# A weights-stationary projection as three 256-column matmuls into a half bank, instead of 512 + 256 columns whose halves are added afterwards

## The chip, the core and the metric

The kernel runs on one core of a Trainium2 chip. The metric is the device time of one execution in microseconds (us); the time before is the median of three runs.

## What is computed

The reference is a two-layer decoder trunk on 256 tokens (`T`) with 2048 features (`D_MODEL`). Layer 0 normalises, multiplies by one wide input matrix, runs an mLSTM head group and an SSD (state-space) head group, and projects back. Layer 1 is causal attention with 16 heads and rotary positions. Each layer ends in a SwiGLU feed-forward network of width 5632. All inputs and outputs are float32.

```python
def swiglu(x, w_gate, w_up, w_down):
    return (jax.nn.silu(x @ w_gate) * (x @ w_up)) @ w_down
...
    proj = (xn @ w_in).astype(f32)                  # layer 0: q, k, v, o, gates, z, x/B/C
...
    qkv = (xn @ w_qkv).astype(jnp.float32)          # layer 1
```

Nearly all the work is in these products `x @ w`.

## The kernel before

**Precision.** Both factors of a product are split into two parts of the type float32r: a high part and the rest. With x = xh + xl and w = wh + wl, the kernel adds three products, wh xh + wh xl + wl xh. The class `KT` (L140 to L158) holds an operand with its features on the partitions; its blocks keep xh and xl of a feature tile side by side, 256 tokens each, so that `both(k)` (L156) is one row of 512 columns [xh | xl] and `parts(k)` (L151) gives the two apart.

**Weights.** `chunk` (L192) brings 2 x 128 rows of a strip of 512 columns of a weight matrix in by DMA from the SP queue (`raw`, 512 KB), has ScalarE (ACT) copy it to `wh` (L202) and VectorE (DVE) subtract to get `wl` (L203). There are four buffers of `raw`, three each of `wh` and `wl`. These two steps are emitted with a raised priority.

**The two forms of a product.** `lin_a` (L234) keeps the activations stationary and moves 512 weight columns per matmul, three matmuls (L247 to L249) per feature tile and token tile. `lin_w` (L206) keeps the weights stationary. It makes a strip of 512 output features in four banks of PSUM, one for each 128 features, over 16 feature tiles k of the input, so it issues 4 x 16 = 64 pairs of matmuls per strip. The first of a pair (L217) multiplies `wh` with the 512 columns [xh | xl] into the whole bank, the second (L219) multiplies `wl` with the 256 columns xh into the first half of the bank:

```python
banks = [acc_bank("acc_w") for _ in range(4)]
...
nc.tensor.matmul(banks[f], wh[:, kk, fs], kt.both(k), start=k == 0, ...)
nc.tensor.matmul(banks[f][:, :T], wl[:, kk, fs], kt.parts(k)[0], start=False, ...)
```

**Reading the sums.** At the end of a strip the two halves of each bank are still to be added. `lin_sum` (L224) copies the second half to SBUF on ACT (L225) and adds the first half on VectorE (L226). `lin_scaled` (L228) does that and multiplies by the norm's factor by token on VectorE (L232).

**Who calls `lin_w`.** 64 strips: four for q and k of layer 0 (L278 and L328), eight in `conv_strip` (L484, four of x and two each of B and C), 44 in the two `ffn` (L626: 11 gate strips, read by `lin_scaled`, and 11 up strips, read by `lin_sum` and a product L648, in each), eight in `rope_strip` (L665, read by `lin_sum`, then by products L673 and L677 with the rotary factors and by the ACT copies L675 and L676 that swap halves).

**The gates.** The 96 gate columns of layer 0 are a product of their own (L343 to L345), weights stationary, 16 feature tiles of `xa`, three matmuls of 256 columns each, all into one half of a bank: `wgh` by xh, `wgh` by xl, `wgl` by xh.

**Order of the work.** PSUM has six banks with the tag `acc` (`psa`, for `lin_w` and `lin_a`) and two with the tag `aux` (for transposes and small products). Small pieces of work (transposes, mLSTM heads, SSD heads, attention heads) are not emitted where they come up: `later` puts them on a list, due some chunks of weights later, and `tick` (L133), called after every chunk, emits what is due. They thus run between the matmuls of the projections. Each engine works its queue in order.

Of the kernel before, what the change touches and what calls it, by code (L numbers as in the profile page):

```python
# [17 lines left out]
P = 128  # L18
T = 256
# [5 lines left out]
KC = 2  # L25
# [28 lines left out]
def hybrid_trunk(ctx: ExitStack, tc: tile.TileContext, a: dict, out: bass.AP):  # L54
# [19 lines left out]
    def acc_bank(name):  # L74
        return psa.tile([P, 512], F32, tag="acc", name=name)
# [45 lines left out]
    def later(wait, name, fn, *args):  # L121
        """Emit fn(*args) behind the next wait chunks of weights."""
        pending.append((clock[0] + wait, len(pending), name, fn, args))
# [16 lines left out]
    class KT:  # L140
        """Features on partitions, split in two float32r parts, 4 tiles of 128 features to a block."""

# [17 lines left out]
    def transpose_split(kt, b, src, gcol, half):  # L160
        """src[t]: [128 tokens, 512 features] -> half of block b of kt, times the gains."""
        blk_ = kt.block(b)
        pt = aux_bank("p_tr")
        for j in range(2):
            for t in range(NT):
                c = (2 * half + j) * P
                nc.tensor.transpose(pt[:, j * T + t * P:j * T + (t + 1) * P], src[t][:, c:c + P], ident)  # L167
        for j in range(2):
            k = 2 * half + j
            split(blk_[:, k, 0, :], blk_[:, k, 1, :], pt[:, j * T:(j + 1) * T],  # L170
                  pv[:, gcol + 4 * b + k:gcol + 4 * b + k + 1])
# [5 lines left out]
    def row_norm(name, ss4):  # L177
        """r [128, 2] by token, 0.5 r, and r over the free dimension on all partitions [128, 256]."""
        ss = sml.tile([P, NT], F32, tag="ss", name="ss" + name)
        nc.vector.tensor_reduce(ss, ss4, axis=AX.X, op=OP.add)  # L180
        r = cst.tile([P, NT], F32, name="r" + name)
        rsqrt_mean(r, ss, D)
        pb = aux_bank("p_rb")
        for t in range(NT):
            dg = t2([P, P], "dg")
            nc.vector.tensor_scalar(dg, ident, r[:, t:t + 1], None, op0=OP.mult)
            nc.tensor.matmul(pb[:, t * P:(t + 1) * P], ones, dg, start=True, stop=True)
        rb = cst.tile([P, T], F32, tag="rb", name="rb" + name, bufs=2)
        nc.scalar.copy(rb, pb[:, :T])
        return r, rb  # L190

    def chunk(w, k, col, step=KC):  # L192
        """KC x 128 rows of a strip of w in two float32r parts, brought in and split step x 128 rows at a time."""
        raw = stg.tile([P, KC, STRIP], F32, tag="raw", name="raw", bufs=4)
        wh = stg.tile([P, KC, STRIP], F32R, tag="wh", name="wh")
        wl = stg.tile([P, KC, STRIP], F32R, tag="wl", name="wl")
        for i in range(0, KC, step):
            ks = slice(i, i + step)
            nc.sync.dma_start(raw[:, ks, :],
                              w[(k + i) * P:(k + i + step) * P, col:col + STRIP].rearrange("(a p) f -> p a f", p=P))  # L200
            with tc.high_priority(offset=800):
                nc.scalar.copy(wh[:, ks, :], raw[:, ks, :])  # L202
                nc.vector.tensor_sub(wl[:, ks, :], raw[:, ks, :], wh[:, ks, :].bitcast(F32))  # L203
        return wh, wl

    def lin_w(w, col, kt, nk, ready=None):  # L206
        """Weights stationary: a bank for 128 features, [w x_hi | w_hi x_lo], which adds up to [128, 256 tokens]."""
        banks = [acc_bank("acc_w") for _ in range(4)]
        for k0 in range(0, nk, KC):
            wh, wl = chunk(w, k0, col, KC if ready is None or k0 else 1)  # L210
            if ready is not None:
                ready(k0)
            for f in range(4):
                fs = slice(f * P, (f + 1) * P)
                for kk in range(KC):
                    k = k0 + kk
                    nc.tensor.matmul(banks[f], wh[:, kk, fs], kt.both(k), start=k == 0, stop=False,  # L217
                                     skip_group_check=True)
                    nc.tensor.matmul(banks[f][:, :T], wl[:, kk, fs], kt.parts(k)[0], start=False, stop=k == nk - 1,  # L219
                                     skip_group_check=True)  # L220
            tick()
        return banks

    def lin_sum(bank, dst):  # L224
        nc.scalar.copy(dst, bank[:, T:])  # L225
        nc.vector.tensor_add(dst, bank[:, :T], dst)  # L226

    def lin_scaled(bank, dst, rb):  # L228
        """dst = the product, times a factor by token."""
        s = t2([P, T], "ls")  # L230
        lin_sum(bank, s)
        nc.vector.tensor_mul(dst, s, rb)  # L232

    def lin_a(w, col, kt, nk, lead=1):  # L234
        """Activations stationary: [128 tokens, 512 features] in a bank per token tile."""
        banks = [acc_bank("acc_a") for _ in range(NT)]
# [19 lines left out]

    # ------------------------------------------------------------ layer 0 input
    w_in = a["l0_w_in"]
# [25 lines left out]
    nc.vector.tensor_scalar(rh0, r0_, 0.5, None, op0=OP.mult)  # L284
    for f in range(4):
        lin_scaled(banks_q[f], qT[:, f, :], rb0)

    # ------------------------------------------------------------ small parameters
    mask_sl = cst.tile([P, P], F32, name="mask_sl")
# [35 lines left out]

    # ------------------------------------------------------------ q, k
    for dst, c0, s in ((qT, C_Q, 1), (kT, C_K, 0), (kT, C_K, 1)):
        banks = lin_w(w_in, c0 + s * STRIP, xt0, KD)  # L328
        for f in range(4):
            lin_scaled(banks[f], dst[:, 4 * s + f, :], rb0)  # L330

    # ------------------------------------------------------------ gates
    wg = blk([P, KD, 96], "wg")
# [65 lines left out]
    def decay_rows(first):  # L399
        """Rows first .. first + 3 on all partitions, l in 0:256 and 128:256 again, masked on the diagonal blocks."""  # L400
        rb = blk([P, 4, W3], "rows4")
# [9 lines left out]
    def decay(row, bias):  # L411
        """exp(row[l] + bias[s]) for s <= l, 0 elsewhere: [128 s, (s tile 0: 256 l | s tile 1: 128 l)]."""
        e = t2([P, W3], "dec")
        nc.scalar.activation(e[:, :T], row[:, :T], AF.Exp, bias=bias[0])
        nc.scalar.activation(e[:, T:], row[:, T:], AF.Exp, bias=bias[1])
        return e

    # ------------------------------------------------------------ mLSTM
    v = [blk([P, MH, MDV + 1], f"v{t}") for t in range(NT)]
# [62 lines left out]

    # ------------------------------------------------------------ SSD
    def conv_strip(col, dst):  # L484
        """dst: [128 channels, 4, 256] <- silu(conv) of 512 channels."""
        banks = lin_w(w_in, C_X + col, xt0, KD)
        for b in range(2):
            xr = t2([P, 2, T + 3], "xr")
            nc.gpsimd.memset(xr[:, :, 0:3], 0.0)
            for j in range(2):  # L490
                lin_scaled(banks[2 * b + j], xr[:, j, 3:], rb0)
            cv = t2([P, 2, T], "cv")
# [112 lines left out]

    # ------------------------------------------------------------ residual blocks
    xr_ = [blk([P, D], f"xres{t}") for t in range(NT)]
# [3 lines left out]
    def project_add(w, kt, nk, name, gcol):  # L611
        """x += kt.T @ w; the next layer's operands, strip by strip, and its norm."""
        nx = KT("x" + name, KD)
# [12 lines left out]
    def ffn(xt, rb, wg_, wu_, name):  # L626
# [3 lines left out]
        for s in range(DFF // STRIP):  # L630
            banks = lin_w(wg_, s * STRIP, xt, KD)
            sgs = []
            for b in range(2):
                gs = t2([P, 2, T], "sg")
                sgs.append(gs)
                for j in range(2):
                    lin_scaled(banks[2 * b + j], gs[:, j, :], rbh)
                th = t2([P, 2, T], "thf")
# [5 lines left out]
            for b in range(2):  # L644
                ur = t2([P, 2, T], "ur")
                for j in range(2):
                    lin_sum(banks[2 * b + j], ur[:, j, :])
                nc.vector.tensor_mul(ur, ur, sgs[b])  # L648
                split(hb[:, 2 * b:2 * b + 2, 0, :], hb[:, 2 * b:2 * b + 2, 1, :], ur)
# [5 lines left out]

    # ------------------------------------------------------------ attention
    rope = cst.tile([P, 2, T], F32, name="rope")
# [7 lines left out]
    def rope_strip(col, name):  # L665
        banks = lin_w(w_qkv, col, xt2, KD)
        dst = blk([P, 4, T], name)
        for b in range(2):
            src = t2([P, 2, T], "rsrc")
            for j in range(2):  # L670
                lin_sum(banks[2 * b + j], src[:, j, :])
            d2 = dst[:, 2 * b:2 * b + 2, :]
# [61 lines left out]

    # ------------------------------------------------------------ last projection and norm
    gf = blk([P, D], "gf")
# [46 lines left out]
```

## Time and profile before

| | us |
|---|---|
| median of 3 runs | 2677.27 (2677.26 to 2678.13) |
| profiled execution, span from first to last instruction | 2676.2 |
| PE (TensorE matmuls) busy | 2655.2, 13765 matmuls |
| PEld (TensorE weight loads) busy | 2250.8, 13765 loads |
| DVE (VectorE) busy | 1621.3 |
| ACT (ScalarE) busy | 1334.3 |
| POOL (GpSimd) busy | 45.9 |

The profile gives the profiled execution's own time as its span, 2676.2 us; the median of the runs lies 1.1 us above it. Busy time is the time in which an engine had at least one instruction in work. Matmuls are pipelined: a matmul's record begins when it starts and ends when its modelled passage through the array is over, so records of neighbours overlap. The time from one start to the next shows the pace. Rows of a group of instructions read: line, engine, operation, what it writes `<-` what it reads, shapes, count | busy us, mean ns of one | idle time of the engine before them, and what ended it.

### The profile page before, as it was taken

The numbers are of one execution on the slowest core, as the hardware profiler recorded it, in microseconds if no ns is written. First come the engines' busy times: TensorE is split into PE (matmuls) and PEld (weight loads), VectorE is DVE, ScalarE is ACT, GpSimd is POOL, SyncE is SP. The second block draws the span as 40 slices with busy tenths as digits, with TensorE's granted clock in tenths as the row PEclk, the third lists the DMA queues.
The fourth block names the chain that finished last, engine by engine and source line by source line (L and its number), as shares of the span: only waits on it lengthen the run. The fifth ranks groups of instructions, "written<-read, shape, count | busy, mean of one in ns | idle before, by whom it ended". The sixth has DMA issues, their size and how long they took to land.

```text
span 2676.2 us, 35559 instructions
## 1 busy us (share of the span) xinstructions
PE 2655.2 (99%) x13765; PEld 2250.8 (84%) x13765; DVE 1621.3 (61%) x2128; ACT 1334.3 (50%) x1906; POOL 45.9 (2%) x97
## 2 busy tenths in 40 slices
PE   8999999999999999999999999999999999999998
PEld 7888888888888888888888888888888888888886
DVE  5675687755456666666544466566566666665454
ACT  5455665665444444444444455556444444444343
POOL 1000010000000000000000000000000000000000
PEclk9999999999999999999999999999999999999999
DMA  7566666566556666666655565554566666666664
GB/s 229 168 191 179 187 182 203 162 186 213 186 184 182 188 189 187 185 188 188 189 187 187 186 181 173 173 174 157 181 186 190 190 190 189 189 189 204 189 189 157
DMA packets 254344, 496.84 MB, mean 186 GB/s; under 512 B 15656, under 2 KB 16048, under 8 KB 253792
## 3 DMA queue, kind: packets, MB, share of 16 engines
q1 hardware_dynamic: 250816, 484.57, 60.2%
q0 software_dynamic: 2896, 8.51, 1.2%
q8 instruction: 107, 1.75, 0.3%
q10 hardware_dynamic: 464, 1.52, 0.2%
q14 instruction: 61, 0.50, 0.1%
HBM read 492.39 MB, written 2.14 MB: 185 GB/s over the span
## 4 chain that ended last, share of the span: by engine, by line
PE 98%; DVE 1%; DMA 1%; ACT 0%; issue 0%; POOL 0%; SPq 0%; ACTq 0%; POOLq 0%; DVEq 0%
PE acc_w L217 35%; PE acc_w L219 18%; PE acc_a L247 14%; PE acc_a L248 14%; PE acc_a L249 14%; PE p_tr L167 1%; PE p_y L572 1%; PE p_num L449 0%; DMA raw<-in_l_w_in 0%; DVE wl L203 0%; ACT wh L202 0%; PE p_qk L687 0%; PE p_o L717 0%; DMA xin<-in_x 0%; PE p_pt L709 0%
## 5 line engine op out<-in xcount | busy, mean ns | idle before, releaser
L203 DVE TENSOR_TENSOR wl<-raw,wh 128x1024 fp32r<-128x1024 f32 (+1 forms) x913 | 1117.4, 1224 | 947.8 <-ACT wh L202 944.2
L202 ACT CAST wh<-raw 128x1024 fp32r<-128x1024 f32 (+1 forms) x913 | 957.3, 1049 | 1171.2 <-PE acc_w L217 549.6
L217 PE MATMUL acc_w<-x,wh 128*128 128x512 f32 x3328 | 1168.8, 396 | 0.0
L219 PE MATMUL acc_w<-x,wl 128*128 128x256 f32 x3328 | 931.0, 280 | 0.0
L217 PEld LDWEIGHTS acc_w<-x,wh 128*128 128x128 f32 x3328 | 625.0, 188 | 146.0
L219 PEld LDWEIGHTS acc_w<-x,wl 128*128 128x128 f32 x3328 | 625.7, 188 | 0.5
L217 PE MATMUL acc_w<-xa,wh 128*128 128x512 f32 x768 | 275.5, 401 | 1.1 <-DVE xa L116 1.1
L219 PE MATMUL acc_w<-xa,wl 128*128 128x256 f32 x768 | 217.1, 285 | 0.0
L217 PEld LDWEIGHTS acc_w<-xa,wh 128*128 128x128 f32 x768 | 145.1, 189 | 33.1 <-ACT wh L202 1.5
L247 PE MATMUL acc_a<-wh,xa 128*128 128x512 f32 x384 | 152.9, 398 | 0.0
L248 PE MATMUL acc_a<-wl,xa 128*128 128x512 f32 x384 | 152.7, 398 | 0.0
L249 PE MATMUL acc_a<-wh,xa 128*128 128x512 f32 x384 | 152.3, 397 | 0.0
L219 PEld LDWEIGHTS acc_w<-xa,wl 128*128 128x128 f32 x768 | 145.3, 190 | 1.1
L247 PE MATMUL acc_a<-wh,ha 128*128 128x512 f32 x352 | 139.4, 396 | 0.0
L248 PE MATMUL acc_a<-wl,hb 128*128 128x512 f32 x352 | 139.0, 395 | 0.0
L247 PE MATMUL acc_a<-wh,hb 128*128 128x512 f32 x352 | 138.7, 394 | 0.0
L249 PE MATMUL acc_a<-wh,ha 128*128 128x512 f32 x352 | 138.7, 394 | 0.0
L249 PE MATMUL acc_a<-wh,hb 128*128 128x512 f32 x352 | 138.6, 394 | 0.0
L248 PE MATMUL acc_a<-wl,ha 128*128 128x512 f32 x352 | 138.5, 393 | 0.0
L247 PE MATMUL acc_a<-wh,mx 128*128 128x512 f32 x256 | 101.8, 397 | 0.0
L248 PE MATMUL acc_a<-wl,mx 128*128 128x512 f32 x256 | 101.1, 395 | 0.0
L249 PE MATMUL acc_a<-wh,mx 128*128 128x512 f32 x256 | 101.0, 394 | 0.0
(240 smaller groups left out, 2519.3 us busy)
## 6 DMA issues: line engine op xcount, KB each, us to landing
raw<-in_l_w_in SPq DMA_DIRECT2D x191, 512.0 KB, 3.7
raw<-in_l_ffn_gate SPq DMA_DIRECT2D x176, 512.0 KB, 3.7
raw<-in_l_ffn_up SPq DMA_DIRECT2D x176, 512.0 KB, 3.7
raw<-in_l_ffn_down SPq DMA_DIRECT2D x176, 512.0 KB, 4.4
raw<-in_l_w_qkv SPq DMA_DIRECT2D x96, 512.0 KB, 3.7
raw<-in_l_w_out SPq DMA_DIRECT2D x64, 512.0 KB, 3.8
raw<-in_l_w_o SPq DMA_DIRECT2D x32, 512.0 KB, 3.7
rows<-scr POOLq DMA_DIRECT2D x10, 512.0 KB, 6.4
```

Source lines behind the costliest of these rows:

```text
L167: nc.tensor.transpose(pt[:, j * T + t * P:j * T + (t + 1) * P], src[t][:, c:c + P], ident)
L202: nc.scalar.copy(wh[:, ks, :], raw[:, ks, :])
L203: nc.vector.tensor_sub(wl[:, ks, :], raw[:, ks, :], wh[:, ks, :].bitcast(F32))
L217: nc.tensor.matmul(banks[f], wh[:, kk, fs], kt.both(k), start=k == 0, stop=False, skip_group_check=True)
L219: nc.tensor.matmul(banks[f][:, :T], wl[:, kk, fs], kt.parts(k)[0], start=False, stop=k == nk - 1, skip_group_check=True)
L247: nc.tensor.matmul(banks[t], xh[:, ts], wh[:, kk, :], start=k == 0, stop=False)
L248: nc.tensor.matmul(banks[t], xh[:, ts], wl[:, kk, :], start=False, stop=False)
L249: nc.tensor.matmul(banks[t], xl[:, ts], wh[:, kk, :], start=False, stop=k == nk - 1)
L572: nc.tensor.matmul(py[:, o0:o0 + SHD], e[:, lo:lo + P], y[st][:, hs], start=st == 0, stop=st == t, skip_group_check=True)
```

## The change

`lin_w` takes two banks for a strip instead of four, two groups of 128 features to a bank, one in each half. For each group and feature tile it issues three matmuls of 256 columns into the same half bank: `wh` by xh, `wh` by xl, `wl` by xh. The three products are added in PSUM as they come. `lin_sum` is gone. `lin_scaled` is one VectorE product of 512 columns (two groups of features) that reads the bank; the up strips' product L648 and the rotary products and copies read the bank too. Comments and docstrings that the diff also touches are left out here.

```diff
     def lin_w(w, col, kt, nk, ready=None):
-        banks = [acc_bank("acc_w") for _ in range(4)]
+        banks = [acc_bank("acc_w") for _ in range(2)]
...
             for f in range(4):
                 fs = slice(f * P, (f + 1) * P)
+                o = banks[f // 2][:, (f % 2) * T:(f % 2 + 1) * T]
                 for kk in range(KC):
                     k = k0 + kk
-                    nc.tensor.matmul(banks[f], wh[:, kk, fs], kt.both(k), start=k == 0, stop=False,
+                    xh, xl = kt.parts(k)
+                    nc.tensor.matmul(o, wh[:, kk, fs], xh, start=k == 0 and f % 2 == 0, stop=False,
                                      skip_group_check=True)
-                    nc.tensor.matmul(banks[f][:, :T], wl[:, kk, fs], kt.parts(k)[0], start=False, stop=k == nk - 1,
-                                     skip_group_check=True)
+                    nc.tensor.matmul(o, wh[:, kk, fs], xl, start=False, stop=False, skip_group_check=True)
+                    nc.tensor.matmul(o, wl[:, kk, fs], xh, start=False, stop=k == nk - 1, skip_group_check=True)
             tick()
-        return banks
-
-    def lin_sum(bank, dst):
-        nc.scalar.copy(dst, bank[:, T:])
-        nc.vector.tensor_add(dst, bank[:, :T], dst)
+        return [b.rearrange("p (a b) -> p a b", a=2) for b in banks]
 
     def lin_scaled(bank, dst, rb):
-        s = t2([P, T], "ls")
-        lin_sum(bank, s)
-        nc.vector.tensor_mul(dst, s, rb)
+        nc.vector.tensor_mul(dst, bank, rb[:, None, :].to_broadcast([P, 2, T]))
...
     def conv_strip(col, dst):
-            for j in range(2):
-                lin_scaled(banks[2 * b + j], xr[:, j, 3:], rb0)
+            lin_scaled(banks[b], xr[:, :, 3:], rb0)
...
     def ffn(xt, rb, wg_, wu_, name):
-                for j in range(2):
-                    lin_scaled(banks[2 * b + j], gs[:, j, :], rbh)
+                lin_scaled(banks[b], gs, rbh)
...
-                for j in range(2):
-                    lin_sum(banks[2 * b + j], ur[:, j, :])
-                nc.vector.tensor_mul(ur, ur, sgs[b])
+                nc.vector.tensor_mul(ur, banks[b], sgs[b])
...
     def rope_strip(col, name):
-            src = t2([P, 2, T], "rsrc")
-            for j in range(2):
-                lin_sum(banks[2 * b + j], src[:, j, :])
+            src = banks[b]
```

The four q and k strips of layer 0 are read in the same way, by two `lin_scaled` of 512 columns instead of four of 256.

## Rows read from the trace of the kernel before

**Rows 1.** The page: busy time, share and count by engine; PE clock by slice.
```profile
PE 2655.2 (99%) x13765; PEld 2250.8 (84%) x13765; DVE 1621.3 (61%) x2128; ACT 1334.3 (50%) x1906; POOL 45.9 (2%) x97
...
PEclk9999999999999999999999999999999999999999
```

**Rows 2.** The page: the chain that ended last, shares by engine.
```profile
PE 98%; DVE 1%; DMA 1%; ACT 0%; issue 0%; POOL 0%; SPq 0%; ACTq 0%; POOLq 0%; DVEq 0%
```

**Rows 3.** Waits of PE: who waited for whom, us in total, times, longest.
```profile
PE p_rb L187 <- DVE dg L186: 2.6, 3, 0.9
PE acc_w L217 <- DVE xa L116: 1.1, 1, 1.1
PE p_cols L390 <- ACT colsrc L381: 0.7, 1, 0.7
PE acc_a L247 <- ACT wh L202: 0.5, 1, 0.5
PE p_xs L542 <- DVE xsT L503: 0.2, 1, 0.2
```

**Rows 4.** Groups of instructions on PE, by line and shape.
```profile
L217 PE MATMUL acc_w<-x,wh 128*128 128x512 f32 x3328 | 1168.8, 396 | 0.0
...
L217 PE MATMUL acc_w<-xa,wh 128*128 128x512 f32 x768 | 275.5, 401 | 1.1 <-DVE xa L116 1.1
```

**Rows 5.** Timeline of PE around the gates: start us, us, instruction.
```profile
83.59 0.39 PE L217 MATMUL acc_w<-xa,wh 128*128 128x512 f32 x1
...
105.95 0.28 PE L343 MATMUL p_gate<-xa,wgh 128*96 128x256 f32 x1
...
107.37 0.28 PE L343 MATMUL p_gate<-xa,wgh 128*96 128x256 f32 x1
...
108.76 0.28 PE L343 MATMUL p_gate<-xa,wgh 128*96 128x256 f32 x1
...
109.94 0.28 PE L344 MATMUL p_gate<-xa,wgh 128*96 128x256 f32 x1
...
110.55 0.28 PE L343 MATMUL p_gate<-xa,wgh 128*96 128x256 f32 x1
...
111.60 0.39 PE L217 MATMUL acc_w<-xa,wh 128*128 128x512 f32 x1
...
122.89 0.40 PE L217 MATMUL acc_w<-xa,wh 128*128 128x512 f32 x1
```

**Rows 6.** Timeline of PE in layer 0's feed-forward network, two strip starts.
```profile
820.65 0.39 PE L217 MATMUL acc_w<-x,wh 128*128 128x512 f32 x1
...
843.15 0.39 PE L217 MATMUL acc_w<-x,wh 128*128 128x512 f32 x1
```

**Rows 7.** Weight loads (PEld): timeline at 336 us, then two groups.
```profile
336.43 0.76 PEld L572 LDWEIGHTS p_y<-y,dec 128*128 128x128 f32 x6
337.10 0.19 PEld L217 LDWEIGHTS acc_w<-xa,wh 128*128 128x128 f32 x1
...
L248 PEld LDWEIGHTS acc_a<-wl,xa 128*128 128x128 f32 x384 | 72.2, 188 | 15.7
L247 PEld LDWEIGHTS acc_a<-wh,xa 128*128 128x128 f32 x384 | 72.2, 188 | 15.9
```

**Rows 8.** DMA queue of PE's instructions: packets, MB, share of 16 engines.
```profile
q8 instruction: 107, 1.75, 0.3%
```

**Rows 9.** Groups of instructions on ACT and DVE that read sums.
```profile
L225 ACT COPY ls<-acc_w 128x256 f32<-128x256 f32 x136 | 48.4, 365 | 6.9 <-PE acc_w L219 6.9
...
L226 DVE TENSOR_TENSOR ls<-acc_w,ls 128x256 f32<-128x256 f32 x136 | 55.1, 418 | 0.0
...
L648 DVE TENSOR_TENSOR ur<-ur,sg 128x512 f32<-128x512 f32 x44 | 30.2, 687 | 0.8
...
L232 DVE TENSOR_TENSOR sg<-ls,rbha 128x256 f32<-128x256 f32 x44 | 18.6, 424 | 1.1
...
L619 DVE TENSOR_TENSOR xres<-xres,acc_a 128x512 f32<-128x512 f32 x24 | 15.4, 681 | 0.0
```

More of the change, by code (lines that the diff above doesn't have):

```diff
@@ L284, in hybrid_trunk @@
     nc.vector.tensor_scalar(rh0, r0_, 0.5, None, op0=OP.mult)
-    for f in range(4):
-        lin_scaled(banks_q[f], qT[:, f, :], rb0)
+    for b in range(2):
+        lin_scaled(banks_q[b], qT[:, 2 * b:2 * b + 2, :], rb0)
     mask_sl = cst.tile([P, P], F32, name="mask_sl")
@@ L328, in hybrid_trunk @@
         banks = lin_w(w_in, c0 + s * STRIP, xt0, KD)
-        for f in range(4):
-            lin_scaled(banks[f], dst[:, 4 * s + f, :], rb0)
+        for b in range(2):
+            lin_scaled(banks[b], dst[:, 4 * s + 2 * b:4 * s + 2 * b + 2, :], rb0)
     wg = blk([P, KD, 96], "wg")
```

## The prediction

> **What bounds the kernel now.** I began with the page. TensorE is busy for 2655.2 of 2676.2 us and its clock is granted in full in every slice [rows 1]; the chain of work that ended last is 98% PE, 1% DVE and 1% DMA [rows 2]. A busy PE need not be a PE at its peak, so I next asked what it waits for. The waits that ACT or VectorE end are small: 2.6 us in three waits on `dg`, 1.1 on `xa`, 0.7 on `colsrc`, 0.5 on `wh`, 0.2 on `xsT`, 5.1 us in all [rows 3]; beside them that list has only two waits on input transfers at the very start. So the end is set by how fast PE takes its matmuls, and only that pace is worth reading closely.
>
> The changed code is that of 4096 pairs (3328 + 768), each a 512-column and a 256-column matmul on one bank [rows 4]. The durations there (396 and 401 ns) overlap and their ends are modelled, so the pace has to be read from starts. On layer 0's operand `xa`, the 64 pairs of a whole strip run from 83.59 to 105.95 us: 22.36 / 64 = 349.4 ns a pair. The next strip's first 32 pairs take 122.89 - 111.60 = 11.29 us, 352.8 ns a pair [rows 5]. In the feed-forward network of layer 0, 64 pairs take 22.50 us, 351.6 ns each [rows 6]. The same work thus differs by 3 ns from place to place.
>
> **The change part by part.**
>
> *The matmuls.* 512 + 256 columns become 3 x 256: the same 768 columns, but one more matmul and one more weight load per pair, 4096 of each. The kernel already has this form: the gates (L343 to L345) multiply hi by hi, hi by lo and lo by hi, 256 columns each, into one half bank. Their 16 triples run from 105.95 to 111.60 us: 5.65 / 16 = 353.1 ns [rows 5]. The moving tiles are the very same `xa`; only the weights are 96 columns wide instead of 128. Against the strip before, a triple is 353.1 - 349.4 = 3.7 ns dearer; against the mean of both neighbours, (349.4 + 352.8) / 2 = 351.1, it is 2.0 dearer. I take the middle, 2.8 ns: 4096 x 2.8 = **11.5 us more**, all on the path, since PE is the path. The ends: the gates' fastest four triples (107.37 to 108.76) take 347.5 ns each, 1.9 less than the strip before, which gives 4096 x -1.9 = -7.8 us; their slowest four (105.95 to 107.37) take 355.0, 5.6 more, +22.9 us [rows 5].
>
> The Trainium skill, page "TensorE: Matmul & The Clock Gate", section "Wait — 56ns, not 53.3ns?", says that every matmul costs some 2.5 ns beyond its columns at the full clock. By it the split would cost 4096 x 2.5 = 10.2 us, an estimate of that page; the 2.0 to 3.7 ns above agree with it.
>
> *The third load.* A load of 128 columns is recorded at 188 ns, but loads overlap in the record. Where they set the pace, before 64-column matmuls, six start between 336.43 and 337.10 us, one every 112 ns [rows 7]. A 256-column matmul takes 353.1 / 3 = 117.7 ns, so a load still fits behind each, with 6 ns to spare where a 512-column matmul left 120. I cost it at nothing; the cover is thin, and the second rival below is what it costs if it is gone. The loads of one weight tile for two matmuls in a row are not merged now either: L247 and L248 use the same tile of `xa` and record 384 loads each [rows 7].
>
> *Fetching instructions.* The 8192 added PE instructions have to be brought in, beside 2 x 13765 now [rows 1]: 30% more. All that the instruction queue q8 moves takes 0.3% of the DMA engines' time in 107 packets [rows 8]; 30% of that is 0.1%, and I cost it at nothing. No queue of data transfers gains, loses or moves an entry.
>
> *Reading the sums.* Each of the 64 strips loses four ACT copies of a half bank (L225), 256 in all, 256 x 0.365 = 93 us, and as many VectorE adds (L226), 256 x 0.418 = 107 us. The 136 products of 256 columns (L232) become 68 of 512 that read the bank; a 512-column VectorE operation on a bank takes 681 ns (L619), so 136 x 0.424 - 68 x 0.681 = 11 us fewer [rows 9]. The others (L648, L673, and ACT's L675 and L676) keep their sizes and read PSUM instead of SBUF; I bound that at nothing, as L619, which reads a bank, costs what L648 costs now (687 ns) [rows 9]. VectorE loses some 118 us and ACT 93 us, all beside PE. What can come back on the path is only part of the waits of [rows 3]. The `dg` waits stand behind layer norms that no changed line feeds, and the `xa` wait precedes the first evacuation; 0.7 us on `colsrc` and 0.2 on `xsT` come from queues that get shorter. The ends are 0 and 5.1 us (all five waits); I take 0.5 us.
>
> *The banks.* A strip holds two banks instead of four, of six. No wait for a bank stands among PE's waits [rows 3], so I cost the relief at nothing. Each bank is read after its second half is done, about two pairs' work later for its first half; the reader still has the rest of the strip's last chunk and a further strip of some 22 us before that bank is needed.
>
> **The sum.** 11.5 - 0.5 = +11.0 us on a span of 2676.2, which makes 2687.2. The runs' median, 2677.27, lies 1.1 us above that span, so the time is 2677.3 + 11.0 = **2688 us**, 0.4% slower.
>
> **The rivals.**
>
> *Columns alone set the pace* (chance 0.13). If a matmul costs its columns and nothing else, 3 x 256 costs what 512 + 256 does and only the 0.5 us remain: about 2677 us. For it: the strip behind the gates runs at 352.8 ns, only 0.3 below the triple. Against it: the strip before them, on the same operand.
>
> *Loads come late* (0.07). With 6 ns to spare, a load that is held up stalls PE at once. In the gates' rows the slowest five matmuls in a row start 0.61 us apart in sum (109.94 to 110.55), 122 ns each [rows 5]. Were that the pace everywhere, a triple would take 366 ns, 15 more than 351.1: +61 us, 2738 us. It decides where a load needs over 118 ns. Against it: the gates show this stretch once in 48, and 128-column loads were seen at 112 ns.
>
> *Loads bound PE by their recorded length* (0.01). At 188 ns a load one after another, a triple takes 564 ns: 4096 x 215 ns = 879 us more, 3556 us. Against it: the six loads ahead of the 64-column matmuls would need 6 x 188 = 1128 ns and pass in 670 [rows 7].
> The Trainium skill, page "Perfetto Trace Analysis", section "Identifying the Most-Contended Engine", judges TensorE's headroom by the share of time that weight loads are busy, which speaks against adding a third load to each pair. By that rule the time would be that rival's; the trace disagrees, since the recorded loads overlap.
>
> *The short matmuls run faster* (0.07), the one that ends below. The place is PE's 4096 triples: if all ran as the gates' fastest four (347.5 ns), each would be 1.9 ns cheaper, and the time 2677.3 - 7.8 - 0.5 = 2669 us. It decides from 1.2 ns cheaper on (4.9 us and the 0.5). For it: that block of rows. Against it: the other twelve triples take 355.0 each (105.95 to 107.37 and 108.76 to 111.60) [rows 5].
>
> **How the numbers follow.** A measurement of this kernel can tell about 0.2% from no change, 5.4 us: 2671.9 to 2682.7. The forecast has 0.72. Its own range goes from 1.5 ns a triple, just outside that band, to 5.6 ns (2700); 0.04 of it I give to ends within the band. So slower is 0.68 + 0.07 + 0.01 = 0.76, same 0.04 + 0.13 = 0.17, faster 0.07. The range takes in the forecast up to its upper bound of 2700 and the rival of columns alone, 2676 to 2701; it leaves out the fast rival and both load rivals, 0.15.
>
> **What the changed profile would show.** Right: 4096 matmuls more on PE, all of 256 columns in `lin_w`, each starting some 117 to 119 ns after the last, so the strips that now take 22.36 and 22.50 us last about 0.2 longer; ACT some 93 us and VectorE some 118 us less busy; the chain still 98% PE; waits as now. Wrong: a strip as long as now (columns alone) or shorter; starts 122 ns apart or more (loads); new waits of PE on a reader of `acc_w`, which would be a cost I have not priced; or a time that moves while the strips do not.

## The result, and the profile after

The changed kernel takes 2700.11 us (median of 4 runs, 2699.37 to 2701.63); the kernel before, run beside it, 2677.37 us (4 runs, 2677.26 to 2678.13). The ratio is 1.0085, with a 95% interval of 1.0071 to 1.0099: 22.7 us slower, 0.85%. The forecast was 2688 us in a range of 2676 to 2701. The direction holds, the time lies at the upper end of the range, and the loss is twice the 11 us that the sum gave.

The page of the kernel after, with the lines that answer to [rows 1, 2, 4, 7 and 8]: busy time, PE's granted clock by slice, the queue of instructions, the chain by engine, and groups of matmuls and weight loads (busy us, mean ns of one, idle us before them).

```profile
PE 2676.5 (99%) x17861; PEld 2454.1 (91%) x17861; DVE 1523.8 (56%) x1804; ACT 1248.0 (46%) x1650; POOL 45.7 (2%) x97
...
PEclk9999999999999999999999999999999999999999
...
q8 instruction: 139, 2.28, 0.3%
...
PE 94%; DVE 0%; ACT 0%; issue 0%; POOL 0%; ACTq 0%; POOLq 0%; DVEq 0%
...
L219 PE MATMUL acc_w<-x,wh 128*128 128x256 f32 x3328 | 939.5, 282 | 0.0
...
L222 PEld LDWEIGHTS acc_w<-x,wl 128*128 128x128 f32 x3328 | 631.7, 190 | 0.0
```

PE has the 4096 added matmuls and loads, at a clock granted in full. The chain is still PE's, with 94% where the prediction had 98%; the line gives almost nothing of the rest to any other engine. VectorE is 97.5 us less busy and ACT 86.3 us less, and the end has moved out all the same. The waits of PE that answer to [rows 3] (who waited for whom, us in total, times, longest) are these:

```profile
PE p_rb L187 <- DVE dg L186: 2.6, 3, 0.9
PE acc_w L219 <- ACT wh L202: 1.1, 1, 1.1
PE p_cols L386 <- ACT colsrc L377: 1.0, 1, 1.0
PE acc_a L243 <- ACT wh L202: 0.5, 1, 0.5
PE acc_w L221 <- DVE xa L116: 0.5, 1, 0.5
```

They sum to 5.7 us against 5.1 before, and none is on a reader of `acc_w`. So neither a new wait nor a vanished one explains the time; PE's pace does. Where it was lost is read from the starts of the same strips in both timelines (start us, us, instruction). First the kernel before: first strip of layer 0's feed-forward network, first of attention, first of layer 1's network, two strips of that network, and its last strip.

```profile
795.75 0.40 PE L217 MATMUL acc_w<-x,wh 128*128 128x512 f32 x1
...
1540.53 0.40 PE L217 MATMUL acc_w<-x,wh 128*128 128x512 f32 x1
...
1930.22 0.40 PE L217 MATMUL acc_w<-x,wh 128*128 128x512 f32 x1
...
1977.13 0.39 PE L217 MATMUL acc_w<-x,wh 128*128 128x512 f32 x1
...
1999.37 0.39 PE L217 MATMUL acc_w<-x,wh 128*128 128x512 f32 x1
...
2399.57 0.39 PE L217 MATMUL acc_w<-x,wh 128*128 128x512 f32 x1
```

The kernel after, the same places, with the two strips of layer 0's network that [rows 6] show of before as second and third row:

```profile
796.72 0.28 PE L219 MATMUL acc_w<-x,wh 128*128 128x256 f32 x1
...
821.71 0.28 PE L219 MATMUL acc_w<-x,wh 128*128 128x256 f32 x1
...
844.49 0.28 PE L219 MATMUL acc_w<-x,wh 128*128 128x256 f32 x1
...
1547.70 0.28 PE L219 MATMUL acc_w<-x,wh 128*128 128x256 f32 x1
...
1939.36 0.28 PE L219 MATMUL acc_w<-x,wh 128*128 128x256 f32 x1
...
1987.43 0.28 PE L219 MATMUL acc_w<-x,wh 128*128 128x256 f32 x1
...
2010.24 0.28 PE L219 MATMUL acc_w<-x,wh 128*128 128x256 f32 x1
...
2420.76 0.28 PE L219 MATMUL acc_w<-x,wh 128*128 128x256 f32 x1
```

After is late by 1.0 us where layer 0's network begins, by 7.2 at attention, 9.1 at layer 1's network and 21.2 at its last strip; the spans differ by 21.3. So the mixer lost 1.0 us, layer 0's network 6.2, attention 2.0 and layer 1's network 12.0. The two networks do the same work and lose unequally. A strip is 64 pairs or triples, so its length over 64 is the pace. Layer 0: 22.50 us became 22.78, that is 351.6 ns a pair and 355.9 a triple. Layer 1: 22.24 became 22.81, 347.5 ns and 356.4. The triples cost nearly the same in both; it was the pairs of layer 1 that had been faster. Why they had been, no run shows.

### The profile page after: what moved, and what is told of

Same layout as the page of the kernel before. It is cut to its first block, busy times and chain, and to the rows that moved or that the text cites. A ratio compares the mean times of both kernels' runs of the same rounds, so it can differ in the third digit from the quotient of the medians.

```text
span 2697.5 us, 43172 instructions
## 1 busy us (share of the span) xinstructions
PE 2676.5 (99%) x17861; PEld 2454.1 (91%) x17861; DVE 1523.8 (56%) x1804; ACT 1248.0 (46%) x1650; POOL 45.7 (2%) x97
## 4 chain that ended last, share of the span: by engine, by line
PE 94%; DVE 0%; ACT 0%; issue 0%; POOL 0%; ACTq 0%; POOLq 0%; DVEq 0%
PE acc_w L219 17%; PE acc_w L222 16%; PE acc_w L221 16%; PE acc_a L243 14%; PE acc_a L244 14%; PE acc_a L245 14%; PE p_y L567 1%; PE p_tr L167 1%; PE p_num L445 0%; PE p_qk L677 0%; PE p_o L707 0%; ACT wh L202 0%; DVE wl L203 0%; PE p_pt L699 0%; PE p_o L708 0%
## 5 line engine op out<-in xcount | busy, mean ns | idle before, releaser
L219 PE MATMUL acc_w<-x,wh 128*128 128x256 f32 x3328 | 939.5, 282 | 0.0
L221 PE MATMUL acc_w<-x,wh 128*128 128x256 f32 x3328 | 935.7, 281 | 0.0
L219 PEld LDWEIGHTS acc_w<-x,wh 128*128 128x128 f32 x3328 | 630.0, 189 | 0.5
L221 PEld LDWEIGHTS acc_w<-x,wh 128*128 128x128 f32 x3328 | 629.6, 189 | 0.5
L219 PE MATMUL acc_w<-xa,wh 128*128 128x256 f32 x768 | 219.5, 286 | 1.1 <-ACT wh L202 1.1
L221 PE MATMUL acc_w<-xa,wh 128*128 128x256 f32 x768 | 216.6, 282 | 0.5 <-DVE xa L116 0.5
L219 PEld LDWEIGHTS acc_w<-xa,wh 128*128 128x128 f32 x768 | 145.3, 189 | 2.0 <-ACT wh L202 1.5
L221 PEld LDWEIGHTS acc_w<-xa,wh 128*128 128x128 f32 x768 | 145.4, 189 | 1.2 <-DVE xa L116 0.7
```

The costliest lines, as they stand in the source:

```text
L219: nc.tensor.matmul(o, wh[:, kk, fs], xh, start=k == 0 and f % 2 == 0, stop=False, skip_group_check=True)
L221: nc.tensor.matmul(o, wh[:, kk, fs], xl, start=False, stop=False, skip_group_check=True)
```

## The experiments

All paces below are strip lengths over 64, from the two strips named in each fence or from the same two strips of each network; means over a block (16 triples of a strip) are from the same starts. Each change of code is against the kernel named.

**1. The split alone** (before, matmuls split, banks and reading kept).

```diff
-                    nc.tensor.matmul(banks[f], wh[:, kk, fs], kt.both(k), ...)
+                    xh, xl = kt.parts(k)
+                    nc.tensor.matmul(banks[f][:, :T], wh[:, kk, fs], xh, ...)
-                    nc.tensor.matmul(banks[f][:, :T], wl[:, kk, fs], kt.parts(k)[0], ...)
+                    nc.tensor.matmul(banks[f][:, T:], wh[:, kk, fs], xl, ...)
+                    nc.tensor.matmul(banks[f][:, :T], wl[:, kk, fs], xh, ...)
```

> The kernel before with one edit: three matmuls of 256 columns (wh xh and wl xh into the first half bank, wh xl into the second), four banks, the copy and the add kept. Theory A (the whole difference is TensorE's pace, a 256-column triple with three loads against a pair with two): as slow as the changed kernel, 2698 to 2701 us, ratio to before 1.008 to 1.009. Rival B (the split itself costs the 2.8 ns a triple of the prediction and the rest comes from reading the sums out of PSUM or from the shared half banks): 2687 to 2690 us, ratio 1.004.

Measured: 2702.06 us (2701.37 to 2702.53), ratio 1.0091 [1.0076, 1.0107]. The whole loss is there with every copy and add still in place; a strip of layer 1's network takes 22.81 us, as in the kernel after. Half banks, fewer banks and lighter readers have no part in the loss; the kernel after lies 2 us below this one, and the two intervals overlap.

**2. The lighter reading alone** (before, pairs kept; the sum read by one VectorE copy).

```diff
 def lin_sum(bank, dst):
-    nc.scalar.copy(dst, bank[:, T:])
-    nc.vector.tensor_add(dst, bank[:, :T], dst)
+    nc.vector.tensor_copy(dst, bank[:, :T])
```

> The kernel before with the pairs kept and the add of the second half left out: the sum is read as a VectorE copy of the first half bank alone, so the product with the low part of the activations is missing from the result, and ACT's 256 copies are gone. Theory A (reading the sums lies beside TensorE): within 0.1% of before, 2675 to 2678 us. Rival B (lighter reading brings the path something): 2672 us or less.

Measured: 2677.60 us (2676.42 to 2679.32), ratio 1.0000 [0.999, 1.0009]. The page shows ACT 82 us lighter than [rows 1], and no gain:

```profile
PE 2653.9 (99%) x13765; PEld 2250.3 (84%) x13765; DVE 1616.3 (60%) x2128; ACT 1252.0 (47%) x1650; POOL 45.8 (2%) x97
```

So what the change saves on ACT lies beside the path. VectorE, whose add became a copy, is only 5 us lighter here; that its 97.5 us lie beside the path too is read from PE's waits. That part of the sum, 0.5 us, was right to be small.

**3. Narrower loads** (the kernel after; second and third matmul load 64 columns of weights).

```diff
-                    nc.tensor.matmul(o, wh[:, kk, fs], xl, ...)
-                    nc.tensor.matmul(o, wl[:, kk, fs], xh, ...)
+                    nc.tensor.matmul(o[:64], wh[:, kk, fn], xl, ...)    # fn: the first 64 of fs
+                    nc.tensor.matmul(o[:64], wl[:, kk, fn], xh, ...)
```

> The changed kernel, where the second and third matmul of each triple load 64 weight columns instead of 128, so that half of the rows of those two products are missing from the result. Theory A1 (each load delays the stream that it runs beside, in proportion to its columns): triples 4 to 8 ns faster than in the changed kernel (356.5 ns in layer 1's feed-forward network), total 2676 to 2688 us. Theory A2 (the pace is that of the stream of 256 columns plus a fixed price for each matmul, and loads play no part): no change, 2697 to 2702 us. Theory A3 (loads of 128 columns set the pace): matmuls before a narrow load start 110 ns or less apart, total below 2670 us.

Measured: 2681.27 us, one run. As many matmuls, loads and moved columns as in the kernel after, and 19 us of the 22.7 are gone. Two strips of layer 0's network and two of layer 1's in the timeline:

```profile
843.28 0.28 PE L220 MATMUL acc_w<-x,wh 128*128 128x256 f32 x1
...
865.68 0.28 PE L220 MATMUL acc_w<-x,wh 128*128 128x256 f32 x1
...
1998.21 0.28 PE L220 MATMUL acc_w<-x,wh 128*128 128x256 f32 x1
...
2020.69 0.28 PE L220 MATMUL acc_w<-x,wh 128*128 128x256 f32 x1
```

22.40 and 22.48 us, 350.0 and 351.3 ns a triple, against 355.9 and 356.4. So the third matmul and its moved columns as such are not what costs most; the loss goes with the width of the two products. The edit halves two things at once, the weight columns that are loaded beside the stream and the rows of the bank that are written, and nothing here tells them apart; what follows calls it the loads, as the forecast did. A1's pace and time hold, A2 and A3 miss.

**4. Fewer moved columns** (the kernel after; second and third matmul move 128).

```diff
-                    nc.tensor.matmul(o, wh[:, kk, fs], xl, ...)
-                    nc.tensor.matmul(o, wl[:, kk, fs], xh, ...)
+                    nc.tensor.matmul(o[:, :P], wh[:, kk, fs], xl[:, :P], ...)
+                    nc.tensor.matmul(o[:, :P], wl[:, kk, fs], xh[:, :P], ...)
```

> The changed kernel, where the second and third matmul of each triple move 128 columns instead of 256, so that those products are missing for half of the tokens. It shows how fast loads of 128 columns can follow each other. Theory A1 or A2 (the stream sets the pace at 256 columns): the next matmul starts 108 to 112 ns after a short one, the load's own pace, clearly under the 117 to 120 ns of now; a triple then takes about 118 + 2 x 111 = 340 ns, total about 2630 to 2640 us. Theory A3 (loads set the pace): the starts stay 117 to 120 ns apart and the time within 0.2% of the changed kernel.

Measured: 2685.79 us, one run. The triple of about 340 ns of A1 and A2 comes, but no forecast's time does. Its timeline in layer 1's network (start us, us, instruction):

```profile
2010.03 0.33 PE L219 MATMUL acc_w<-x,wh 128*128 128x256 f32 x1
2010.20 0.22 PE L221 MATMUL acc_w<-x,wh 128*128 128x128 f32 x1
2010.26 0.27 PE L222 MATMUL acc_w<-x,wl 128*128 128x128 f32 x1
2010.37 0.34 PE L219 MATMUL acc_w<-x,wh 128*128 128x256 f32 x1
```

The starts are 170, 60 and 110 ns apart: 340 ns for 512 moved columns, where 768 take 356. A third less is moved, and three loads of 128 columns still take 113.3 ns each, a triple 340 to 342 in every block of the two networks; I take that for their own pace, beside the 112 ns of [rows 7]. The loads of the kernel after come every 356.4 / 3 = 118.8, so they are not bound by that pace. The time does not fall below the kernel after's by as much as the strips promise because the mixer is longer here (waits of 6.8 us on `colsrc`, 6.5 on `cT`, 6.3 on `dg` and 3.2 on `xsT` in all; the granted clock is 0.94 in the first 400 us and 1.00 after, 0.989 over the span). That part of the run I do not use.

**5. The pair with a narrower second load** (before).

```diff
-                    nc.tensor.matmul(banks[f][:, :T], wl[:, kk, fs], kt.parts(k)[0], ...)
+                    nc.tensor.matmul(banks[f][:64, :T], wl[:, kk, f * P:f * P + 64], kt.parts(k)[0], ...)
```

> The kernel before, where the second matmul of each pair loads 64 weight columns instead of 128, so that half of the rows of the product with the weights' low part is missing from the result. Theory A (a pair or triple costs 340 ns for 768 moved columns and some 0.0435 ns for each weight column loaded beside them: 350.2 ns for the pair with 256, 351.7 for the narrowed triple with 256, 353.1 for the gates' triple with 288, 356.7 for the changed triple with 384): 192 loaded columns, 348.4 ns a pair, 1.8 ns less on average, total 2669 to 2672 us. Rival C (each matmul has a fixed price and loads cost nothing beside a 512-column one): no change, 2676 to 2679 us.

Measured: 2670.67 us, one run, within the forecast. Pairs too get cheaper when the second product is narrower (in loaded columns and written rows), but not everywhere alike: the mean pair falls from 351.5 to 349.4 ns in layer 0's network and only from 347.4 to 347.0 in layer 1's.

Up to here one line fitted the means of whole kernels to 1 or 2 ns: 340 ns for 768 columns, and some 5.6 ns for each 128 columns of weights loaded (351 for a pair, 357 for a triple). Layer 1's pairs, at 347.5, lie 4 ns off it, and the next seven runs show that the second number is no constant. Within a strip of the kernel after, the pace changes with the block of activations that moves, and the blocks differ in one thing, where they lie in SBUF. By the layout, weight tiles start at 32 bytes past a multiple of 128 in both kernels, and blocks come every 8224 bytes (the same slots hold `v`, 8 x 257 floats), so that they start 0, 32, 64 or 96 past one. The following edits move tiles and compute the same; the temporary tiles move with the blocks. The diff of experiments 10 and 12 follows, with remarks added and without the lines that open the pads' pools, fill the pads and cut `v` to its columns; the others differ from it in the two pads, in the slot of `v` and in the buffers of `tmp`:

```diff
+    shw = gpw.tile([P, 8], F32, name="shw")        # weights 32 bytes further
+    shift = gap.tile([P, 48], F32, name="shift")   # activation blocks 192 further
-    v = [blk([P, MH, MDV + 1], f"v{t}") for t in range(NT)]
+    v = [blk([P, MH, MDV + 8], f"v{t}") for t in range(NT)]     # slots of 8448 bytes
-    tmp = ctx.enter_context(tc.tile_pool(name="tmp", bufs=9))
+    tmp = ctx.enter_context(tc.tile_pool(name="tmp", bufs=7))
```

**6. Every block at the weights' remainder** (the kernel after; blocks every 8320 bytes, no pads).

> The changed kernel, where all the blocks that hold the activations lie at the same place modulo 128 bytes as the weight tiles (blocks 8320 bytes apart instead of 8224, one temporary buffer fewer). In the changed kernel the four blocks of each operand lie at four different places and run at 340 to 360 ns a triple. Theory D (how much a load delays a stream depends on where the two tiles lie to each other): all blocks run alike, and as slowly as those that share the weights' place now, 358 to 360 ns, total 2706 to 2716 us. Theory E (place plays no part): 356 to 357 ns on average, total 2698 to 2702 us, and the blocks differ as now.

Measured: 2702.66 us, one run; the strips take 22.90 and 22.97 us, 357.8 and 358.9 ns a triple. The blocks come closer without becoming alike, and what tells them apart is the remainder modulo 256: in the two networks blocks at the weights' own remainder take 359 to 360 ns, those 128 bytes from it 356. In the kernel after the blocks at the weights' remainder modulo 256 are the slowest too, 359 to 360 ns, with the others at 352 to 356. Theory D's time misses its range, since the pace is only 2 ns above the 355.9 and 356.4 of the kernel after; theory E's ends 0.7 us below the measured time.

**7. Aligned, changed** (weights at 64 past a multiple of 128, blocks at multiples of 128).

> The changed kernel, where weight tiles start at a multiple of 64 bytes (64 modulo 128) and all activation blocks at a multiple of 128. Theory D: all blocks run alike, at another pace than in the kernel with one common place; if the load's delay comes from tiles that straddle 64-byte units, the triple falls to 340 ns or below, total 2635 us or less; if only from the two tiles' distance, 340 to 355 ns, total 2640 to 2695 us. Theory E: 2698 to 2702 us.

Measured: 2676.03 us, one run, 24 us under the kernel after with the same matmuls, loads and transfers. In the timeline, a strip of layer 0's network, then one of layer 1's:

```profile
840.57 0.28 PE L225 MATMUL acc_w<-x,wh 128*128 128x256 f32 x1
...
862.77 0.28 PE L225 MATMUL acc_w<-x,wh 128*128 128x256 f32 x1
...
1991.65 0.28 PE L225 MATMUL acc_w<-x,wh 128*128 128x256 f32 x1
...
2014.26 0.28 PE L225 MATMUL acc_w<-x,wh 128*128 128x256 f32 x1
```

22.20 us is the mean of two paces: in layer 0's strips the triples of a block take either 340 or 353 ns. The 22.61 us of layer 1 are 353.3 ns throughout.

**8. Aligned, before** (the same places, pairs).

> The kernel before with the same places of weights and activations as in the aligned changed kernel. Theory D: its pairs run alike in all blocks, 340 to 347 ns, total 2640 to 2665 us, and it stays ahead of the aligned changed kernel by what the third load still costs. Theory E: 2676 to 2679 us.

Measured: 2688.66 us, one run. The forecast of 2640 to 2665 fails: these places make the pairs slower, 22.60 and 22.59 us a strip, 353 ns a pair, and within 2 ns of that in every block. A place that suits triples need not suit pairs.

**9. The aligned changed kernel, timed.**

> The aligned changed kernel once more, timed: whether its 2676.0 us of one look is below the kernel before (2677.3). If its pace is fixed by the places, it repeats within 3 us and the verdict is 0.999 to 1.001 of before; if the pace depends on where the phases of weights and stream happen to fall in an execution, its runs spread over more than 5 us.

Measured: 2670.84 us (10 runs, 2668.97 to 2675.45), ratio to before 0.9976 [0.9967, 0.9985]. It does beat the kernel before, by 0.2%. Its runs spread over 6.5 us (four of them at 2674.0 to 2675.5, six at 2669.0 to 2671.3), where those of before spread over 1.3: at these places the time is not fully fixed by the program. What differs from run to run I did not find.

**10 and 11. All blocks at 128 past a multiple of 256, and all at 0** (changed kernel). In experiment 7 the blocks of layers 0 and 1 at 128 past 256 had been the fast ones, with one exception.

> The changed kernel, nothing left out; only places in SBUF differ: weight tiles start at 64 past a multiple of 128 bytes as in the aligned changed kernel, and every activation block now starts at 128 past a multiple of 256 bytes (blocks 8448 bytes apart; one temporary buffer fewer). Theory M (a block's place modulo 256 decides: in the aligned changed kernel the blocks of layers 0 and 1 that lay at 128 past 256 ran at 340 ns a triple, those at 0 at 353): all triples 340 to 342 ns, 4096 x (356.7 - 341) = 64 us under the changed kernel, 2630 to 2645 us, faster than both. Theory N (the place matters, but by something else than this remainder; one block at 128 past 256 ran at 353 there): triples remain a mixture of 340, 353 and 360 ns and the time 2665 to 2700.

> The same with every activation block at a multiple of 256 bytes, the temporary buffers as many; nothing left out. Theory M: all triples 353 ns, 4096 x (356.7 - 353.3) = 14 us under the changed kernel, about 2686 us, some 50 above the kernel with the blocks at 128 past 256. Theory N: a mixture again, within 15 us of that kernel.

Measured: **2631.35 us** (4 runs, 2629.66 to 2633.12), ratio to before 0.9823 [0.9806, 0.9839], for 128; 2694.81 us, one run, for 0. The two programs differ by 128 bytes of padding, and by 63 us; the first is 1.8% faster than the kernel before and 2.5% faster than the change as made (2631.35 / 2700.11). The timeline of the first (a strip of layer 0's network, then one of layer 1's with the starts of a triple):

```profile
836.21 0.28 PE L225 MATMUL acc_w<-x,wh 128*128 128x256 f32 x1
...
857.97 0.28 PE L225 MATMUL acc_w<-x,wh 128*128 128x256 f32 x1
...
1967.39 0.28 PE L225 MATMUL acc_w<-x,wh 128*128 128x256 f32 x1
1967.50 0.28 PE L227 MATMUL acc_w<-x,wh 128*128 128x256 f32 x1
1967.62 0.28 PE L228 MATMUL acc_w<-x,wl 128*128 128x256 f32 x1
1967.73 0.28 PE L225 MATMUL acc_w<-x,wh 128*128 128x256 f32 x1
...
1989.15 0.28 PE L225 MATMUL acc_w<-x,wh 128*128 128x256 f32 x1
```

The second, the same strips:

```profile
844.95 0.28 PE L225 MATMUL acc_w<-x,wh 128*128 128x256 f32 x1
...
867.57 0.28 PE L225 MATMUL acc_w<-x,wh 128*128 128x256 f32 x1
...
1985.69 0.28 PE L225 MATMUL acc_w<-x,wh 128*128 128x256 f32 x1
...
2008.31 0.28 PE L225 MATMUL acc_w<-x,wh 128*128 128x256 f32 x1
```

21.76 us and 340.0 ns a triple in both networks, against 22.62 us and 353.4: theory M's paces to the nanosecond there, and the times that N gave are missed. But the remainder does not decide alone. In the mixer of the first, with weights and blocks at the same remainders, two strips start here:

```profile
61.87 0.28 PE L225 MATMUL acc_w<-xa,wh 128*128 128x256 f32 x1
...
84.48 0.28 PE L225 MATMUL acc_w<-xa,wh 128*128 128x256 f32 x1
```

22.61 us, 353.3 ns a triple. Three of its twelve strips run so throughout and one at 340 ns, the others change between the two, and of all the mixer's triples about half take each. In the kernel at 0 some one in seven of the mixer's triples takes 340. So the same two paces occur at both places, and the place sets which of them holds in the networks and in most of attention; what sets it in the mixer is not found. The sum for the kernel at 0 missed by 9 us (2694.8 for 2686). Part of it is the matmuls of `lin_a`, which the forecast left alone: their mean distance is 233.3 ns there, 232.2 in the kernel after and 229.1 with the blocks at 128, and there are 4800 of them.

**12. The kernel before at the places of experiment 10.**

> The kernel before with the places of the fastest kernel (weights at 64 past a multiple of 128, every activation block at 128 past a multiple of 256), nothing left out: is that kernel's gain the place's or the change's? Theory P (the place alone: where the loads do not disturb the stream 768 columns take 340 ns, in two matmuls or three): pairs 340 ns, 4096 x (350.2 - 340.2) = 41 us under the kernel before, 2630 to 2640 us, as fast as the changed kernel at these places. Theory Q (which places suit depends on the form of the matmuls; in the aligned kernel before all pairs ran at 353 ns, also in the blocks at 128 past 256): pairs 353 ns again, 2683 to 2693 us, so that at these places the change is worth some 55 us.

Measured: 2676.61 us (10 runs, 2675.79 to 2677.78), ratio to before 0.9996 [0.9987, 1.0006]. Two strips of layer 1's network:

```profile
1971.35 0.40 PE L223 MATMUL acc_w<-x,wh 128*128 128x512 f32 x1
...
1993.97 0.40 PE L223 MATMUL acc_w<-x,wh 128*128 128x512 f32 x1
```

22.62 us, 353.4 ns a pair: theory Q's pace. Its time misses on the low side (2676.6 for 2683 to 2693), because `lin_a`'s matmuls gain here too, 229.0 ns for 232.1, which is 4800 x 3.1 = 15 us, as much as the pairs lose, 4096 x (353.4 - 350.2) = 13 us (350.2 is the mean pair of the kernel before). So at these places the change is worth 2676.61 - 2631.35 = 45.3 us, where at the old ones it costs 22.7. The 44 strips of the two networks give 44 x 64 x (353.4 - 340.0) = 37.7 us of it. By the starts in the two timelines attention gives 5 us more, and the mixer, with its many triples at 353 ns, under 1.

## Why the prediction was right, and its size wrong

*What bounds the kernel.* Right. PE's pace set the end before and after; no experiment moved the time through ACT, VectorE or a wait.

*The matmuls* ("I take the middle, 2.8 ns: 4096 x 2.8 = 11.5 us"). This is the term that was mis-sized; it measured 22.7 / 4096 = 5.5 ns, just inside the upper end of 5.6 that the same rows gave. Both of its inputs came from one place. The gates' triple of 353.1 ns stood for all triples, which take 355.9 to 356.4 in the networks. And the pairs beside the gates, 351.1, stood for all pairs, while layer 1's network, a third of the pairs, ran at 347.5; the trace of before held that stretch, and neither the rows nor the sum used it. In layer 0's network the difference is 4.3 ns, in layer 1's 8.9.

By the 2.5 ns a matmul that the Trainium skill, page "TensorE: Matmul & The Clock Gate", section "Wait — 56ns, not 53.3ns?", gives, the loss would be 10.2 us, an estimate of that page and less than half of what was measured. The trace does not bear out a fixed price for each matmul as the cause: three matmuls take 356 ns, 350 with narrower loads (experiment 3) and 340 at other places (experiment 10), where two take 353 (experiment 12).

*The third load* ("so a load still fits behind each ... I cost it at nothing"). It fits, by experiment 4, 113.3 ns for a load in a matmul of 118.8; a pace of 122 does not show as that of a whole strip. But a load that fits need not be free: at the old places, halving the width of two of the three products, loads and written rows together, takes 5 to 6 ns from a triple. Here the step asked only whether the load was late, not whether it slowed the stream. What the loads cost at the places of experiment 10 no run shows: there is none with narrower loads, and the 340.0 ns of a triple are as long as three loads took in experiment 4.

The same page of the Trainium skill, section "Step-by-step: what each phase is for", says that PE reads weights and moving data through two ports of their own, so that a load takes no bandwidth from the matmul that runs. Experiments 3, 10 and 11 do not bear out that a load beside the stream costs it no time: the pace changed with the width of what is loaded (and written), and with where the tiles lie. Whether bandwidth is what the stream loses no run shows.

*Reading the sums, banks, instructions.* Right, each near nothing: experiments 1 and 2, and 32 more packets on q8 at the same 0.3%. VectorE and ACT lost 97.5 and 86.3 us, for 118 and 93 foretold, beside the path.

*What was luck.* The direction. The price came from the gates, whose weights are 96 columns wide and lie, by the layout, at other remainders modulo 256 than the 128-column ones. That a triple is dearer than a pair holds at the old places; at those of experiment 10 the same change is 45.3 us faster, and no row of the prediction could tell the two apart.

*The rivals.* Columns alone, late loads and loads of recorded length did not come: the busy share of the weight loads rose from 84% to 91% with the time 0.85% up, and it is 91% as well in the kernel of experiment 10, 1.8% under before. The fast rival, triples quicker than pairs, failed at the old places and is what happens at the new ones, at seven times its price (13.4 ns for 1.9).

## What to carry to other kernels

A price read from one stretch holds for that stretch; before it is multiplied by 4096, read the pace of the same instruction in every stage, and where it differs from stage to stage find out why first. When an instruction stream is bound by PE's pace, two versions should be compared at more than one placement of their tiles, or a change can be dropped for the padding beside it: this one is 0.85% slower or 1.7% faster. Where loads stand beside every matmul, ask what their width and their place do to the pace, also when they fit.

## What was not expected of the hardware

The time of a program with the same matmuls, loads and transfers went from 2631 to 2703 us by where tiles start in SBUF (experiments 6, 7, 10 and 11, and the kernel after). In both networks the 256-column matmuls showed 113.3 ns (340.0 a triple) at one placement and 117.8 (353.4) at another, at the same granted clock of 0.999. With the weights at 64 past a multiple of 128, blocks at 128 past a multiple of 256 gave the first and blocks at 0 the second there; in the mixer both paces occur at either. What in the chip does this no run shows; nor is it settled why pairs stay at 353 at both, why the mixer changes between the two paces, why one block of experiment 7 at 128 past 256 ran at 353, or whether other weight places would do better still.
